# A hybrid decoder layer on one core: low halves of w_up and w_down formed by an accumulating transfer

## The chip, the core and the metric

One core of one Trainium2 chip. The metric is the device time of one execution in microseconds; the kernel before takes 1103.26 us (median of 2 runs, 1103.16 to 1103.37).

## What is computed

One layer on 256 tokens of width 2048, all in float32: a pooling mixer and sparse attention, an output projection, and a gated feed-forward network with a causal convolution of width 3. The part that the change touches is the last:

```python
def conv_ffn(h, w_up, conv_w, conv_b, w_down):      # w_up 2048 x 11264, w_down 5632 x 2048
    up = h @ w_up
    ...
    c = conv_b + sum(conv_w[j] * up_p[:, j:j + S] for j in range(CONV_WIDTH))
    gate, val = jnp.split(c, 2, axis=-1)
    return (jax.nn.silu(gate) * val) @ w_down
```

## The kernel before

Every weight and every activation is split into a high half, its value rounded to the narrower float32r, and a low half, the difference. A product is the sum of high x high, low x high and high x low. The weights come as a stream of 384 pieces of mostly [128, 1024] float32 (512 KB), two to a unit that one transfer from SP loads into a tile `raw` (1 MB, two buffers). `Piece.split` makes the halves: ACT copies `raw` into `whi`, rounding (L103), DVE subtracts `whi` from `raw` into `wlo` (L104). Both have four buffers, so the halves of piece n use the buffers of piece n-4 and have to wait until that piece's products are done.

The main loop (L735 to L744) goes through the pieces in order. At step i it asks for the load of the unit of piece i+3, splits piece i+2 (`prep`), does the side work of the step (L740) and then the products of piece i. A framework turns this order into one instruction list for each engine, with semaphores between them; it may put instructions of one engine into another order than the code has, as long as the data allow it. Each engine works through its list in order, and so does the queue of transfers that SP issues.

The pieces from G0 = 120 to 295 are w_up: for each f of 44 a unit of gate columns and a unit of value columns, four pieces in all; products at L211 and L212. Side work in each round of four pieces: `up_out` takes the sums out of the accumulators (L613 to L615), `up_conv` does the convolution and the Silu (L623 to L626), `up_gate` forms the gated value and its halves (L631 to L633). The pieces from D0 = 296 to 383 are w_down, 44 units, with the same product lines (for the last two blocks of outputs L216 to L218) and nearly no side work. GpSimd has nothing to do in either stage but the norm's small steps at the start of w_up.

Of the kernel before, what the change touches and what calls it, by code (L numbers as in the profile page):

```python
# [11 lines left out]
AF = mybir.ActivationFunctionType  # L12
ALU = mybir.AluOpType
AX = mybir.AxisListType

P = 128
S = 256
# [10 lines left out]

# columns of the packed parameters
C_AG, C_FG, C_PS, C_QG, C_KG, C_IC, C_CW, C_CB = 0, 16, 32, 40, 41, 42, 58, 58 + 3 * 2 * NF  # L30
C_N = C_CB + 2 * NF

# the indexer's columns: heads (with the key and the head weights in the first chunk)
IHEADS = (5, 6, 5)
IWIDTH = (5 * 64 + 80, 6 * 64, 5 * 64)
# pool groups, the widest window first
GROUPS = (3, 2, 1, 0)
# the columns of w_in: indexer, keys, queries, values, pool groups
ORDER = ("i0", "i1", "i2", "k0", "k1", "u0", "q0", "q1", "u1", "v0", "u2", "v1", "u3")
# [4 lines left out]
def hybrid_kernel(ctx, tc, xT, par, wI0, wI1, wI2, wA, wU, wP, wO, wUp, wDn, out):  # L44
    nc = tc.nc
# [11 lines left out]

# [1 line left out]
    warm = cp.tile([P, 512], BF16, name="warm")  # L59
# [8 lines left out]
    nc.gpsimd.memset(ones, 1.0)  # L68
    # loads the table of functions
    tab = cp.tile([P, 1], F32, name="tab")  # L70
# [3 lines left out]

# [1 line left out]
    class Unit:  # L76
        """Columns of weights that are loaded together."""

# [3 lines left out]
        def load(self):  # L82
            if self.raw is None:
                self.raw = wp.tile([P, 2048], F32, name="raw", tag="raw", bufs=2)
                for i, (a, b) in enumerate(self.cuts):
                    if i == 1 and self is pieces[0].unit:
                        nc.scalar.dma_start(ga, par[:, C_AG:C_AG + KT])
                        nc.sync.dma_start(xf[:, 0:2], xT[:, 0:2])
                    nc.sync.dma_start(self.raw[:, a:b], self.src[:, a:b])

    class Piece:
        """Columns a .. b of a unit, split together, and the products that use them."""

        def __init__(self, unit, a, b, mm):
            self.unit, self.a, self.b, self.mm = unit, a, b, mm

        def split(self, parts=1):
            self.hi = wp.tile([P, 1024], F32R, name="whi", tag="whi", bufs=4)
            self.lo = wp.tile([P, 1024], F32R, name="wlo", tag="wlo", bufs=4)
            n = (self.b - self.a) // parts  # L100
            for c in range(0, n * parts, n):
                raw, hi = self.unit.raw[:, self.a + c:self.a + c + n], self.hi[:, c:c + n]
                i1 = nc.scalar.activation(hi, raw, AF.Copy)  # L103
                i2 = nc.vector.tensor_tensor(self.lo[:, c:c + n], raw, hi.bitcast(F32), op=ALU.subtract)  # L104
                self.issued = i1.ins, i2.ins
# [4 lines left out]
    pieces = []  # L110
    sides = {}

    def at(step, f, *a):
        sides.setdefault(step, []).append(lambda: f(*a))

# [1 line left out]
    def split_x(k, src, gains, on_act):  # L117
# [16 lines left out]

# [1 line left out]
    def rsqrt_cols(pool, src, n, mul, name):  # L136
# [6 lines left out]
    class TokenNorm:  # L143
        """From a [P, S] sum of squares over features: r by token, as columns and along rows."""

# [27 lines left out]
    def squares(q):  # L173
        # not ahead of the first pieces
        act, dve = pieces[7].issued
        with tc.issue_after(act), tc.issue_after(dve):
            nc.scalar.activation(sqz[:, 0], xf[:, 4 * q:4 * q + 4], AF.Square)
            nc.vector.tensor_reduce(sqz[:, 1, q], sqz[:, 0].rearrange("p k t -> p t k"), axis=AX.X, op=ALU.add)  # L178
# [3 lines left out]

# [1 line left out]
    class Acc:  # L184
        """Accumulators [P, 2, 512] or [P, 512], taken when the first product is traced."""

# [10 lines left out]
    def mm_tok(acc, piece, ks, width):  # L197
        """tokens on partitions: acc[:, th, :width] += x[:, k].T @ w[k]."""
        pt = acc.get()
        for i, k in enumerate(ks):  # L200
            wh, wl = piece.get(i * width, width)
            for th in range(2):
                t = slice(th * P, (th + 1) * P)
                o = pt[:, th, :width]
                nc.tensor.matmul(o, xhl[:, k, 0, t], wh, start=(k == 0), stop=False)  # L205
                nc.tensor.matmul(o, xhl[:, k, 0, t], wl, start=False, stop=False)  # L206
                nc.tensor.matmul(o, xhl[:, k, 1, t], wh, start=False, stop=(k == KT - 1))  # L207

    def mm_feat(o, wh, wl, rhs, first, last):
        """features on partitions: o[:, 0:256] += w.T @ hi, + wl.T @ hi; o[:, 256:512] += wh.T @ lo."""  # L210
        nc.tensor.matmul(o, wh, rhs.rearrange("p a t -> p (a t)"), start=first, stop=False)  # L211
        nc.tensor.matmul(o[:, 0:S], wl, rhs[:, 0], start=False, stop=last)  # L212

    def mm_feat1(o, wh, wl, rhs, first, last):
        """The same, all in o[:, 0:256]."""
        nc.tensor.matmul(o[:, 0:S], wh, rhs[:, 0], start=first, stop=False)  # L216
        nc.tensor.matmul(o[:, 0:S], wh, rhs[:, 1], start=False, stop=False)  # L217
        nc.tensor.matmul(o[:, 0:S], wl, rhs[:, 0], start=False, stop=last)  # L218

    def tok_chunk(srcs, width, cuts=()):  # L220
        """16 k-tiles of `width` columns, in units of 4 and pieces of 2 k-tiles."""
        acc = Acc()
        for q in range(4):
            u = Unit(srcs[q], 4 * width, cuts[q] if q < len(cuts) else None)
            for h in range(2):
                def mm(p, k0=4 * q + 2 * h):
                    mm_tok(acc, p, (k0, k0 + 1), width)
                pieces.append(Piece(u, 2 * h * width, (2 * h + 2) * width, mm))
        return acc

    # ================= the stream of pieces =================
    def pool_chunk(n):
# [12 lines left out]
    ia, za, ua, first = [], {}, [], {}  # L245
    W = IWIDTH[0]
    for name in ORDER:
        first[name] = len(pieces)
        if name[0] == "i":
            c = int(name[1])  # L250
            src = (wI0, wI1, wI2)[c]
# [4 lines left out]
        else:  # L256
            c = ("k0", "k1", "q0", "q1", "v0", "v1").index(name)
            za[name] = tok_chunk([wA[c, q] for q in range(4)], 512)

    # rows of w_out: heads 0 .. 3, the first pool groups, heads 4 .. 7, the last pool group  # L260
    yhl = zc.tile([P, KT, 2, S], F32R, name="yhl")
# [27 lines left out]
    G0 = len(pieces)  # L289
# [14 lines left out]
    D0 = len(pieces)  # L304
    ghl = None
    for i in range(16 * NF // 8):
# [10 lines left out]
        o = (i % 2) * 1024  # L317
        pieces.append(Piece(u, o, o + 1024, mm))

    # ================= indexer =================  # L320
    qiT = [zc.tile([P, 8, S], F32R, name=f"qiT{c}", tag="big", bufs=2) for c in range(2)]
# [43 lines left out]
    def tr_iq(h0):  # L365
        """Heads h0 and h0 + 1: [hi; lo] on partitions."""
        tp = ps_s.tile([P, 512], F32, name="tp", tag="ss")
        for a in range(2):
            st, h = qst[h0 + a]
            for th in range(2):  # L370
                nc.tensor.transpose(tp[:, (a * 2 + th) * P:(a * 2 + th + 1) * P],  # L371
                                    st[:, th, h].rearrange("p a d -> p (a d)").bitcast(F32), ident)
        nc.scalar.activation(qiT[h0 // 8][:, h0 % 8:h0 % 8 + 2].rearrange("p a t -> p (a t)"), tp, AF.Copy)
# [33 lines left out]

    # ================= attention =================
    gqk = zc.tile([P, 1], F32, name="gqk")
# [101 lines left out]

    # ================= pool channels: features on partitions =================
    pw_ = {}
# [62 lines left out]

    # ================= x1, its norm =================
    sq1 = cp.tile([P, 2, S], F32, name="sq1")
# [16 lines left out]

    # ================= ConvFFN =================
    fw = {}
# [50 lines left out]

    # ================= what else happens at each piece =================
    at(9, nc.sync.dma_start, pr, par)  # L650
# [58 lines left out]

    # ================= the kernel =================  # L710
    def load(n):
# [11 lines left out]
    def prep(n):  # L723
        if 0 < n < 8:
            for k in (2 * n, 2 * n + 1):
                split_x(k, xf[:, k], ga, True)
        if n < len(pieces):
            pieces[n].split(2 if n == 0 else 1)
        if n == 0:
            for k in range(2):  # L730
                split_x(k, xf[:, k], ga, False)
# [3 lines left out]
    for i, p in enumerate(pieces):  # L735
        if i + 3 < 8:
            load_x(2 * (i + 3))
        load(i + 3)
        prep(i + 2)
        for f in sides.get(i, []):  # L740
            f()
        p.mm(p)
# [59 lines left out]
```

## Time and profile before

| | |
|---|---|
| median of the runs | 1103.26 us |
| span of the profiled execution | 1102.1 us |
| PE busy | 1092.7 us, 99% |
| DVE busy | 734.4 us, 67% |
| ACT busy | 570.0 us, 52% |
| POOL busy | 13.7 us, 1% |
| bytes read from HBM | 201.15 MB |
| granted PE clock | 1.00 throughout |

The profile is one execution, 1.2 us shorter than the median of the runs. A busy time is the sum of the spans of an engine's instructions, so PE, whose matmuls overlap, can be busy without being at its peak. The waits and the order in time say which engine another one waited for; a name such as `wlo` is a tile of the program, and L104 a line of it.

### The profile page before, as it was taken

The page shows a single profiled execution, that of the slowest core. Times are in us where ns is not written, and L with a number is a line of the kernel's source. Part 1 is how long each engine was busy: PE and PEld are TensorE (multiplying, and loading weights), DVE is VectorE, ACT ScalarE, POOL GpSimd, SP SyncE. Part 2 cuts the span into 40 slices and gives each one's busy share as a digit, 9 for nine tenths or more (in the row PEclk, how much of TensorE's full clock was granted, in tenths as well). Part 3 has the DMA queues.
Part 4 walks back from the last instruction along what each step waited for, and adds up shares of the span by engine and source line. Part 5 has one row for each costly group of instructions (what it writes and reads, how often), then busy time and mean ns, then how long its engine had stood idle before and what let it go on. Part 6 is the DMA issues. An engine that isn't in the chain of part 4 may idle for free.

```text
span 1102.1 us, 16427 instructions
## 1 busy us (share of the span) xinstructions
PE 1092.7 (99%) x6620; PEld 974.2 (88%) x6620; DVE 734.4 (67%) x1034; ACT 570.0 (52%) x792; POOL 13.7 (1%) x25
## 2 busy tenths in 40 slices
PE   8999999999999999999999999999999999999998
PEld 6998989889999988888888888888888888888898
DVE  7767867665556677777877787878777544444442
ACT  6555456654444555555555555555555433344441
POOL 0001000000000000000000000000000000000000
PEclk9999999999999999999999999999999999999999
DMA  7554554444555555555555555555555555555552
GB/s 261 165 179 163 191 202 156 163 162 161 181 191 174 175 192 187 191 191 191 191 192 191 191 191 191 192 191 191 190 192 188 188 198 200 197 199 196 198 197 76
DMA packets 31755, 204.30 MB, mean 185 GB/s; under 512 B 3648, under 2 KB 4288, under 8 KB 8640
## 3 DMA queue, kind: packets, MB, share of 16 engines
q1 hardware_dynamic: 30240, 201.16, 53.4%
q10 hardware_dynamic: 1440, 2.11, 0.5%
q8 instruction: 52, 0.85, 0.3%
q14 instruction: 23, 0.19, 0.0%
HBM read 201.15 MB, written 2.10 MB: 184 GB/s over the span
## 4 chain that ended last, share of the span: by engine, by line
PE 96%; DVE 1%; DMA 1%; issue 1%; ACT 0%; SPq 0%; ACTq 0%; DVEq 0%
PE mm L211 43%; PE mm L212 21%; PE mm L218 5%; PE mm L217 5%; PE mm L216 5%; PE mm L206 5%; PE mm L205 5%; PE mm L207 5%; DMA raw<-in_wI_dram 1%; DVE wlo L104 1%; PE sp L381 1%; PE sp L467 0%; DVE sqz L178 0%; PE tp L455 0%; PE tp L371 0%
## 5 line engine op out<-in xcount | busy, mean ns | idle before, releaser
L104 DVE TENSOR_TENSOR wlo<-raw,whi 128x1024 fp32r<-128x1024 f32 (+4 forms) x385 | 462.1, 1202 | 297.4 <-ACT whi L103 297.3
L103 ACT ACTIVATE whi<-raw 128x1024 fp32r<-128x1024 f32 (+4 forms) x385 | 399.9, 1041 | 428.8 <-PE mm L211 260.4
L211 PE MATMUL mm<-xhl,whi 128*128 128x512 f32 x1408 | 488.5, 394 | 0.0
L212 PE MATMUL mm<-xhl,wlo 128*128 128x256 f32 x1408 | 390.1, 277 | 0.0
L211 PEld LDWEIGHTS mm<-xhl,whi 128*128 128x128 f32 x1408 | 264.0, 188 | 61.3
L212 PEld LDWEIGHTS mm<-xhl,wlo 128*128 128x128 f32 x1408 | 264.2, 188 | 0.0
L211 PE MATMUL mm<-ghl,whi 128*128 128x512 f32 x616 | 213.6, 394 | 0.0
L212 PE MATMUL mm<-ghl,wlo 128*128 128x256 f32 x616 | 170.6, 277 | 0.0
L211 PEld LDWEIGHTS mm<-ghl,whi 128*128 128x128 f32 x616 | 115.5, 188 | 26.9
L212 PEld LDWEIGHTS mm<-ghl,wlo 128*128 128x128 f32 x616 | 115.6, 188 | 0.0
L205 PE MATMUL mm<-whi,xhl 128*128 128x512 f32 (+3 forms) x288 | 108.6, 377 | 2.3 <-ACT xhl L120 0.8
L206 PE MATMUL mm<-wlo,xhl 128*128 128x512 f32 (+3 forms) x288 | 107.0, 371 | 2.5 <-DVE wlo L104 2.4
L207 PE MATMUL mm<-whi,xhl 128*128 128x512 f32 (+3 forms) x288 | 106.8, 371 | 0.0
L216 PE MATMUL mm<-yhl,whi 128*128 128x256 f32 x256 | 72.6, 284 | 0.0
L218 PE MATMUL mm<-yhl,wlo 128*128 128x256 f32 x256 | 72.4, 283 | 0.0
L217 PE MATMUL mm<-yhl,whi 128*128 128x256 f32 x256 | 72.4, 283 | 0.0
L206 PEld LDWEIGHTS mm<-wlo,xhl 128*128 128x128 f32 x288 | 54.1, 188 | 10.7 <-DVE wlo L104 4.0
L205 PEld LDWEIGHTS mm<-whi,xhl 128*128 128x128 f32 x288 | 54.1, 188 | 10.5 <-ACT whi L103 1.8
L207 PEld LDWEIGHTS mm<-whi,xhl 128*128 128x128 f32 x288 | 54.1, 188 | 8.3 <-DVE xhl L123 0.5
L217 PEld LDWEIGHTS mm<-yhl,whi 128*128 128x128 f32 x256 | 49.1, 192 | 0.0
L216 PEld LDWEIGHTS mm<-yhl,whi 128*128 128x128 f32 x256 | 49.1, 192 | 0.0
L218 PEld LDWEIGHTS mm<-yhl,wlo 128*128 128x128 f32 x256 | 49.1, 192 | 0.0
(155 smaller groups left out, 928.9 us busy)
## 6 DMA issues: line engine op xcount, KB each, us to landing
raw<-in_wUp_dram SPq DMA_DIRECT2D x88, 1024.0 KB, 4.8
raw<-in_wDn_dram SPq DMA_DIRECT2D x44, 1024.0 KB, 4.8
raw<-in_wA_dram SPq DMA_DIRECT2D x24, 1024.0 KB, 4.8
raw<-in_wO_dram SPq DMA_DIRECT2D x16, 1024.0 KB, 4.8
raw<-in_wU_dram SPq DMA_DIRECT2D x8, 1024.0 KB, 4.8
raw<-in_wI_dram SPq DMA_DIRECT2D x4, 768.0 KB, 4.2
raw<-in_wI_dram SPq DMA_DIRECT2D x7, 400.0 KB, 5.2
raw<-in_wI_dram SPq DMA_DIRECT2D x4, 640.0 KB, 4.1
```

The lines of the kernel that those rows point to most:

```text
L103: i1 = nc.scalar.activation(hi, raw, AF.Copy)
L104: i2 = nc.vector.tensor_tensor(self.lo[:, c:c + n], raw, hi.bitcast(F32), op=ALU.subtract)
L205: nc.tensor.matmul(o, xhl[:, k, 0, t], wh, start=(k == 0), stop=False)
L206: nc.tensor.matmul(o, xhl[:, k, 0, t], wl, start=False, stop=False)
L207: nc.tensor.matmul(o, xhl[:, k, 1, t], wh, start=False, stop=(k == KT - 1))
L211: nc.tensor.matmul(o, wh, rhs.rearrange("p a t -> p (a t)"), start=first, stop=False)
L212: nc.tensor.matmul(o[:, 0:S], wl, rhs[:, 0], start=False, stop=last)
L216: nc.tensor.matmul(o[:, 0:S], wh, rhs[:, 0], start=first, stop=False)
L217: nc.tensor.matmul(o[:, 0:S], wh, rhs[:, 1], start=False, stop=False)
L218: nc.tensor.matmul(o[:, 0:S], wl, rhs[:, 0], start=False, stop=last)
L381: nc.tensor.matmul(sp[:, a:b], q, kiT[:, e, 0:b - a], start=(e == 0), stop=(e == 1))
```

## The change

For every piece n from G0 to D0 + 87 with n mod 4 = 1 (44 of w_up, 22 of w_down; called adder pieces below) the subtraction on DVE is left out. ACT instead writes the negated, rounded copy of `raw` into `wlo`, and GpSimd issues a transfer that adds the float32 weights onto it. For w_up the source of the transfer is `raw` in SBUF, for w_down the same columns in DRAM, read a second time. In the main loop an adder piece is split one step earlier than the others (at step n-3), and before that split the load of the following unit is asked for. Comments of the file are removed as well; those lines are left out here.

```diff
-            self.unit, self.a, self.b, self.mm = unit, a, b, mm
+            self.unit, self.a, self.b, self.mm, self.adder = unit, a, b, mm, None
...
                 i1 = nc.scalar.activation(hi, raw, AF.Copy)
+                if self.adder:
+
+                    nc.scalar.activation(self.lo[:, c:c + n], raw, AF.Copy, scale=-1.0)
+                    src = raw
+                    if self.adder == "dram":
+                        src = self.unit.src[:, self.a + c:self.a + c + n]
+                    nc.gpsimd.dma_start(self.lo[:, c:c + n], src, accum_op=ALU.add)
+                    continue
                 i2 = nc.vector.tensor_tensor(self.lo[:, c:c + n], raw, hi.bitcast(F32), op=ALU.subtract)
...
+    for n in range(G0, D0 + 88):
+        if n % 4 == 1:
+            pieces[n].adder = "sbuf" if n < D0 else "dram"
...
         load(i + 3)
-        prep(i + 2)
+
+        if not (i + 2 < len(pieces) and pieces[i + 2].adder):
+            prep(i + 2)
+        if i + 3 < len(pieces) and pieces[i + 3].adder:
+            load(i + 4)
+            prep(i + 3)
```

## Rows read from the trace of the kernel before

**Rows 1.** The page: span, then busy us and share of each engine.
```profile
span 1102.1 us, 16427 instructions
PE 1092.7 (99%) x6620; PEld 974.2 (88%) x6620; DVE 734.4 (67%) x1034; ACT 570.0 (52%) x792; POOL 13.7 (1%) x25
```
**Rows 2.** Busy us by engine in two stretches, clock, DMA share, GB/s.
```profile
core 0: us, PE busy (x) PEld busy (x) DVE busy (x) ACT busy (x) POOL busy (x), PEclk, DMA share, GB/s
...
354.00:832.00 478.00, 478.00 (x2789) 419.27 (x2788) 362.46 (x511) 272.01 (x385) 1.77 (x3) 1.00 0.55 189
832.00:1095.00 263.00, 263.00 (x1592) 233.42 (x1590) 134.12 (x132) 107.67 (x115) 0.00 (x0) 1.00 0.55 188
```
**Rows 3.** Waits of PE, longest group: us in total, times, longest us.
```profile
PE mm L206 <- DVE wlo L104: 2.4, 4, 1.3
```
**Rows 4.** Line 211: duration ns min/median/max, first and last start us.
```profile
L211 PE MATMUL mm<-xhl,whi x1408: 391/395/476, 364.3 to 853.0; 128*128 128x512 f32 x176
...
L211 PE MATMUL mm<-ghl,whi x616: 392/394/396, 853.4 to 1066.6; 128*128 128x512 f32 x154
```
**Rows 5.** Groups by line, 380 to 1102 us: busy us, mean ns, idle before.
```profile
L104 DVE TENSOR_TENSOR wlo<-raw,whi 128x1024 fp32r<-128x1024 f32 x256 | 313.5, 1225 | 206.9 <-ACT whi L103 206.9
L103 ACT ACTIVATE whi<-raw 128x1024 fp32r<-128x1024 f32 x256 | 271.1, 1059 | 284.0 <-PE mm L211 256.4 <-DMA raw<-in_wUp_dram 13.8 <-PE mm L217 10.2
```
**Rows 6.** ACT in order of time in w_up: start us, us, instruction, idle before.
```profile
598.38 1.06 ACT L103 ACTIVATE whi<-raw 128x1024 fp32r<-128x1024 f32 x1 [1.49 <-PE mm L211]
599.35 0.58 ACT L613 ACTIVATE ft<-mm 128x512 f32<-128x512 f32 x1
601.50 1.06 ACT L103 ACTIVATE whi<-raw 128x1024 fp32r<-128x1024 f32 x1 [1.58 <-DMA raw<-in_wUp_dram]
602.47 1.08 ACT L623 ACTIVATE fc<-up,pr 128x256 f32<-128x256 f32 x2
603.93 1.06 ACT L103 ACTIVATE whi<-raw 128x1024 fp32r<-128x1024 f32 x1 [0.38 <-PE mm L211]
```
**Rows 7.** DVE in the same stretch: the subtraction of the second half.
```profile
605.32 1.22 DVE L104 TENSOR_TENSOR wlo<-raw,whi 128x1024 fp32r<-128x1024 f32 x1
```
**Rows 8.** Loads issued on SP's queue: start us, us of the issue.
```profile
595.18 0.33 SPq L89 DMA_DIRECT2D raw<-in_wUp_dram  x1
...
606.57 0.33 SPq L89 DMA_DIRECT2D raw<-in_wUp_dram  x1
```
**Rows 9.** Transfers by line: count, KB each, median us from issue to landing.
```profile
raw<-in_wUp_dram SPq DMA_DIRECT2D x88, 1024.0 KB, 4.8
...
raw<-in_wI_dram SPq DMA_DIRECT2D x4, 768.0 KB, 4.2
...
out_dram<-ft ACTq DMA_DIRECT2D x7, 256.0 KB, 3.1
...
out_dram<-ft ACTq DMA_DIRECT2D x2, 128.0 KB, 1.8
```
**Rows 10.** The page: SP's queue, packets, MB, share of 16 engines' span.
```profile
q1 hardware_dynamic: 30240, 201.16, 53.4%
```
**Rows 11.** Single microseconds of w_up; the last two columns are DMA share, GB/s.
```profile
603.00:604.00 1.00, 1.00 (x7) 0.89 (x6) 1.00 (x2) 0.62 (x3) 0.00 (x0) 1.00 1.00 426
...
605.00:606.00 1.00, 1.00 (x7) 0.87 (x7) 1.00 (x3) 0.42 (x1) 0.00 (x0) 1.00 0.02 8
```
**Rows 12.** ACT in order of time in w_down, two of a repeating row.
```profile
903.39 1.06 ACT L103 ACTIVATE whi<-raw 128x1024 fp32r<-128x1024 f32 x1 [1.71 <-PE mm L211]
906.16 1.06 ACT L103 ACTIVATE whi<-raw 128x1024 fp32r<-128x1024 f32 x1 [1.71 <-PE mm L211]
```

## The prediction

> **What bounds the kernel now.** I read the busy table first. TensorE (PE) is busy 1092.7 of the 1102.1 us, VectorE (DVE) 67%, ScalarE (ACT) 52%, GpSimd (POOL) 1% [rows 1]. A busy PE is not yet a PE that sets the end, so next come the stretches: from 354 to 832 and from 832 to 1095 us, nearly all of the w_up and w_down stages, PE's busy time equals the stretch to a hundredth, at clock 1.00 [rows 2]. The waits of PE say the same from the other side: its longest group is four waits for a low half, 2.4 us in all [rows 3], and the two stretches hold none of them [rows 2]. So in the two stages that the change touches PE waits for nobody, and the most that a relieved DVE could give back anywhere is 1102.1 - 1092.7 = 9.4 us, 0.9%.
>
> That sets PE's pace. The first product of w_up starts at 364.3 us, the first of w_down at 853.4 [rows 4]: 489.1 us for 176 pieces, 2.78 us a piece, 11.1 us for a round of four. Adder pieces come once a round.
>
> Then I looked for the reserve: how early a piece's halves are made. On ACT a high half takes 1.06 us, the next instruction begins 0.97 us after it began [rows 5, 6]. The copy at 603.93 us is that of the second half of a w_up unit whose first half was copied at 601.50. It had waited for the products four pieces earlier to give its buffer back; its own products begin three pieces later, 603.93 + 3 x 2.78 = 612.3, about. The reserve is 8.3 us, and the old path (copy, then a subtraction that ends at 606.54) uses 2.6 of it [rows 6, 7].
>
> Last, the raw buffers. There are two, and units take turns. SP issues the load of a unit as soon as the subtraction of the unit two before it is done: 606.57 against 606.54 us [rows 7, 8]. A 1 MB load lands 4.8 us after its issue in the median [rows 9]; the one issued at 595.18 landed only as the copy at 601.50 began, 6.3 us later [rows 6, 8]. So a raw buffer goes round load, copy, copy, subtract, load, and this round also comes once in 11.1 us. It is the round that the change lengthens.
>
> **The change, part by part.** *Removed:* 66 subtractions of 1.225 us, 81 us of DVE [rows 5]. In these stages no PE wait names DVE, so this buys nothing.
>
> *Added on ACT:* 66 negated copies of the size of the high-half copy: 66 x 1.06 = 70 us. ACT is busy 272 of 478 us in the w_up stretch [rows 2]; one copy a round makes it about 318. Hidden behind PE as throughput, but it stands in the chain below.
>
> *Added on POOL and the DMA engines:* 66 transfers of 512 KB that read the source, read minus the high half, and write the sum. POOL does next to nothing else in these stages. The engines have room as an average: SP's queue takes 53.4% of them [rows 10]. A load runs in bursts (share 1.00 and 426 GB/s in one microsecond, 8 GB/s two later [rows 11]), so a transfer that falls into a burst is delayed.
>
> *Moved:* an adder piece is split a step earlier and the load of the next unit goes ahead of it on SP. The copies cannot come earlier for that: at 603.93 us ACT was already waiting for PE to release the buffer [rows 6]. What the move does is put copy, copy, negated copy side by side, and keep the other unit's load from queueing behind the transfer.
>
> *The price D of one transfer, issue to landing.* The trace has no accumulating transfer and none issued by POOL, so I bound it. Loads of 768 and 1024 KB land in 4.2 and 4.8 us [rows 9]: 0.6 us per 256 KB, hence 4.8 - 2 x 0.6 = 3.6 us for a plain 512 KB. That is the low end. If the two reads cost what reading 1 MB costs, D = 4.8. If the read of the destination comes first and the rest after it, two plain transfers, D = 7.2; three, with the write apart, 10.8, the high end. I take D = 6.0, midway between 4.8 and 7.2.
>
> The Trainium skill, DMA: Bandwidth & Descriptors, section Anatomy of one DMA — SWDGE (gpsimd) path, fits 2.0 us plus bytes over 436 GB/s; the estimate for 512 KB is 3.2 us, by which the w_up sum below would be 9 us instead of 132. It speaks for the change, and no run shown here has such a transfer. Collectives: The Full Stack (the Trainium skill again), section The bandwidth ceiling, says that a reduction in the DMA engines costs its second read, not its addition; with 1 MB in the same fit the estimate is 4.4 us, and the w_up sum 62 us; no row here shows that either.
>
> *w_up, source in SBUF, 44 rounds.* Here the transfer reads raw, so the raw buffer is free only when it has landed, and the load behind it on SP waits that long; behind that load waits the other unit's load too. The round of the buffer: load 4.8, copies 0.97 + 0.97 + 1.06 = 3.0, three hand-overs of about 0.1 (SP's was 0.03 [rows 7, 8]), transfer D: 8.1 + D. PE's round is 11.1. With D = 6.0 the buffer's round is 14.1 and PE stands 3.0 us in each: 44 x 3.0 = 132 us. The first round eats a reserve of a few microseconds, which I leave out. The two loads go out back to back and are done before the transfer starts, so I add no contention here.
>
> *w_down, source in DRAM, 22 rounds.* Raw is free after the negated copy, at about the old time, so the buffer's round is 8.1 us and hidden. What remains is the reserve: copies for piece n begin when piece n-4 is done (ACT waits 1.71 us each time for just that, every 2.77 us [rows 12]), then 0.97 + 1.06 + 0.2 + D must fit into the 8.3 us until piece n is due: D up to 6.0 is hidden. But the next load is released by the same negated copy and starts beside the transfer. Alone a load keeps the engines for 1 MB / 342 GB/s = 3.1 us (342 = 201.16 MB / (0.534 x 1102.1 us) [rows 1, 10]); the transfer loses between none and all of that; I take half, 1.5. It is then late by 2.2 + 6.0 + 1.5 - 8.3 = 1.4 us: 22 x 1.4 = 31 us.
>
> *Sum* against the profiled execution: 1102.1 + 132 + 31 = 1265; the median of the runs is 1.2 above it: **1266 us**, 15% slower.
>
> **The rivals.** *Not slower: the transfer is short.* One place decides: the raw buffer's round. At D = 3.0 or less it closes within 11.1 us and the time stays 1103. Up to D = 3.5 the loss is 44 x 0.5 = 22 us, which is 2%, about what a measurement of this kernel can tell from no change. For it: a 256 KB store lands in 3.1 us, a 128 KB store in 1.8 [rows 9]. Against it: every load of more than that takes over 4 us, and this one moves 512 KB and reads twice.
>
> *It costs a plain copy.* D = 3.6: the round is 11.7, 44 x 0.6 = 26, w_down hidden: 1130 us. This is what the second read being free would mean. The skill's fit of DMA: Bandwidth & Descriptors, named above, says so or less.
>
> *It is a chain of passes.* D from 7.2 to 10.8, at 9.0: 44 x 6.0 + 22 x (2.2 + 9.0 + 1.5 - 8.3) = 264 + 97, 1464 us; at 10.8 with full contention 44 x 7.8 + 22 x 7.8 = 515, 1618 us. For it: no row prices what POOL does to issue such a transfer, nor how reads and write of one row overlap; against it: the engines moved up to 426 GB/s [rows 11].
>
> Two costs inside these cases: if the two conv steps of L623, 1.08 us together, stand between the ACT copies, as they did at 602.47 [rows 6], 44 x 1.1 = 48 us more; and stops of 3 us could lower PE's clock, which with waits of at most 1.3 us [rows 3] no row shows. In w_up PE is not in the round and has room for it; in w_down a piece at 1.2 instead of 2.4 GHz would add up to 2.8 x 22 = 62 us.
>
> **How the numbers follow.** Transfer of 4.8 to 7.2 us (forecast): 0.55, own range 1185 to 1345 (44 x 1.8 + 22 x 0.2, and 44 x 4.2 + 22 x 2.6). Plain copy to 4.8: 0.12. Chain of passes: 0.20. Short: 0.13, of which 0.01 for a gain beyond 2%, which 9.4 us of PE idle exclude unless the profile misleads. I leave the short case out below and the far third of the chains above (0.07): 1130 to 1500. Faster 0.01, same 0.12, slower 0.87.
>
> **What would show it.** Right: SP's queue in w_up waits for the transfer, ACT waits for a load before the first copy of a unit, PE waits for wlo about 3 us once per four pieces in w_up and less in w_down; issue to landing of the transfers near 6 us. DVE falls by some 81 us, ACT rises by 70. Wrong: D below 3.5 us, or PE waiting as long in w_down as in w_up, which would mean that the transfer itself and not the raw buffer sets the round.

## The result and the profile after

The changed kernel takes 1244.4 us (median of 2 runs), 1.128 times the time before, 95% interval 1.126 to 1.130. The forecast was 1266. The profiled execution spans 1242.7 us, 140.6 more than before.

The page of the changed kernel, busy us and share by engine, the queue of the new transfers, and the chain that ended last:

```profile
span 1242.7 us, 16490 instructions
PE 1130.2 (91%) x6620; PEld 993.1 (80%) x6620; DVE 665.3 (54%) x968; ACT 632.4 (51%) x858; POOL 69.1 (6%) x91
...
q0 software_dynamic: 9504, 34.61, 14.3%
...
DMA 42%; PE 37%; ACT 9%; issue 6%; DVE 4%; SPq 0%; ACTq 0%; DVEq 0%
```

DVE lost 69 us and ACT gained 62 against [rows 1], as the edit says, and neither mattered. The chain that ended last is now made of transfers (loads and additions), 42% of it; before, 96% of it was PE.

The two stretches (w_up, w_down) of the changed kernel; columns as in [rows 2]:

```profile
364.30:937.90 573.60, 517.01 (x2827) 442.33 (x2826) 330.00 (x485) 321.34 (x440) 38.24 (x47) 0.97 0.64 202
937.90:1238.90 301.00, 254.30 (x1496) 222.30 (x1495) 92.19 (x88) 115.45 (x118) 17.92 (x21) 0.99 0.67 191
```

w_up took 489.1 us before [rows 4] and takes 573.6: 84.5 more, 1.92 for each of 44 rounds. w_down went from 245.4 (853.4 to the end of the products) to 301.5: 56.1 more, 2.55 for each of 22. Together 140.6: all of the loss is here, and PE, which had been busy through both stretches, has gaps in both (56.6 and 46.7 us). The rest of the loss is inside PE's busy time, 1130.2 us against 1092.7 for the same 6620 products.

The waits of PE, and of SP's queue in w_up (us in total, times, longest us):

```profile
PE mm L220 <- DMA wlo<-raw: 56.6, 35, 3.1
PE mm L220 <- DMA wlo<-in_wDn_dram: 43.1, 19, 3.4
```

```profile
SPq L89 <- DMA wlo<-raw: 509.1, 43, 13.5
```

PE waits for the transferred low halves: with 3.6 us more at the last lines of w_down, 103.3 us in all. SP, which had waited for subtractions, waits in w_up for transfers, once a round. One round of w_up shows the whole loop; first ACT, then the transfers that POOL issues, then SP's load (start us, us, instruction, what ended the idle time before it):

```profile
606.57 2.01 ACT L103 ACTIVATE whi<-raw 128x1024 fp32r<-128x1024 f32 x2 [1.64 <-DMA raw<-in_wUp_dram]
608.49 1.04 ACT L106 ACTIVATE wlo<-raw 128x1024 fp32r<-128x1024 f32 x1
...
620.57 2.01 ACT L103 ACTIVATE whi<-raw 128x1024 fp32r<-128x1024 f32 x2 [2.92 <-DMA raw<-in_wUp_dram]
```

```profile
609.82 0.86 POOL L110 DMA_DIRECT2D wlo<-raw  x1 [11.88 <-ACT wlo L106]
623.82 0.84 POOL L110 DMA_DIRECT2D wlo<-raw  x1 [13.14 <-ACT wlo L106]
```

```profile
601.64 0.80 SPq L89 DMA_DIRECT2D raw<-in_wUp_dram  x2
...
615.61 0.33 SPq L89 DMA_DIRECT2D raw<-in_wUp_dram  x1
```

Load issued 601.64, copies from 606.57 (4.9 us), negated copy done 609.53 (3.0), transfer issued 609.82 (0.3), next load issued 615.61 as it landed (5.8): 14.0 us. Most rounds are 12.5 to 13.1, with a transfer of 4.3 to 5.0; in nine of the 44, one in five, it lands late like this one, after 5.4 to 6.1 us, and the mean of the 44 is 4.7. Why it does is open. ACT waits for the load before the first copy; its waits for the loads of w_up come to 74.4 us, against 13.8 before [rows 5].

The transfers, KB and median us from issue to landing:

```profile
raw<-in_wUp_dram SPq DMA_DIRECT2D x88, 1024.0 KB, 5.1
raw<-in_wDn_dram SPq DMA_DIRECT2D x44, 1024.0 KB, 5.8
...
wlo<-raw POOLq DMA_DIRECT2D x44, 512.0 KB, 4.4
...
wlo<-in_wDn_dram POOLq DMA_DIRECT2D x22, 512.0 KB, 8.3
```

So D, taken as 6.0 in the forecast, is 4.4 from SBUF with the engines to itself and 8.3 beside loads. The last transfer of w_down, which no load follows, lands in 5.6.

One round of w_down: ACT, the transfer, SP's loads, and PE's wait for the piece:

```profile
1000.97 1.06 ACT L103 ACTIVATE whi<-raw 128x1024 fp32r<-128x1024 f32 x1 [3.84 <-PE mm L219]
1001.93 1.04 ACT L106 ACTIVATE wlo<-raw 128x1024 fp32r<-128x1024 f32 x1
```

```profile
1003.27 0.86 POOL L110 DMA_DIRECT2D wlo<-in_wDn_dram  x1 [12.31 <-ACT wlo L106]
```

```profile
1003.00 0.33 SPq L89 DMA_DIRECT2D raw<-in_wDn_dram  x1
...
1008.80 0.33 SPq L89 DMA_DIRECT2D raw<-in_wDn_dram  x1
```

```profile
1012.08 0.39 PE L220 MATMUL mm<-ghl,wlo 128*128 128x256 f32 x1 [2.54 <-DMA wlo<-in_wDn_dram]
```

The copy waits for PE to give back the buffer of the piece four before. The transfer, issued at 1003.27, lands 8.8 us later, and PE has waited 2.5 us for it. Not one but two loads run beside it: the one issued 0.3 us before it, and the next, issued at 1008.80. So it is with every transfer of the stage but the last.

### The profile page after: what moved, and what is told of

Read it like the earlier page. It is cut to its first block, busy times and chain, and to the rows that moved or that the text cites. A ratio compares the mean times of both kernels' runs of the same rounds, so it can differ in the third digit from the quotient of the medians.

```text
span 1242.7 us, 16490 instructions
## 1 busy us (share of the span) xinstructions
PE 1130.2 (91%) x6620; PEld 993.1 (80%) x6620; DVE 665.3 (54%) x968; ACT 632.4 (51%) x858; POOL 69.1 (6%) x91
## 4 chain that ended last, share of the span: by engine, by line
DMA 42%; PE 37%; ACT 9%; issue 6%; DVE 4%; SPq 0%; ACTq 0%; DVEq 0%
DMA raw<-in_wUp_dram 15%; DMA wlo<-in_wDn_dram 12%; DMA wlo<-raw 12%; PE mm L219 6%; ACT whi L103 5%; PE mm L226 4%; PE mm L224 4%; PE mm L225 4%; PE mm L214 4%; PE mm L213 4%; PE mm L215 4%; ACT wlo L106 4%; PE mm L220 4%; DVE wlo L112 3%; DMA raw<-in_wDn_dram 2%
## 5 line engine op out<-in xcount | busy, mean ns | idle before, releaser
L112 DVE TENSOR_TENSOR wlo<-raw,whi 128x1024 fp32r<-128x1024 f32 (+4 forms) x319 | 381.0, 1197 | 446.4 <-ACT whi L103 445.2
L103 ACT ACTIVATE whi<-raw 128x1024 fp32r<-128x1024 f32 (+4 forms) x385 | 394.0, 1037 | 393.9 <-PE mm L219 162.8
L219 PE MATMUL mm<-xhl,whi 128*128 128x512 f32 x1408 | 507.4, 403 | 0.0
L220 PE MATMUL mm<-xhl,wlo 128*128 128x256 f32 x1408 | 404.8, 288 | 56.6 <-DMA wlo<-raw 56.6
L220 PEld LDWEIGHTS mm<-xhl,wlo 128*128 128x128 f32 x1408 | 272.4, 193 | 68.4 <-DMA wlo<-raw 68.2
L219 PEld LDWEIGHTS mm<-xhl,whi 128*128 128x128 f32 x1408 | 270.7, 192 | 62.8
L220 PE MATMUL mm<-ghl,wlo 128*128 128x256 f32 x616 | 175.2, 284 | 43.1 <-DMA wlo<-in_wDn_dram 43.1
L631 ACT ACTIVATE fc<-up,pr 128x256 f32<-128x256 f32 x88 | 48.1, 594 | 94.0 <-DVE up L623 94.0
L110 POOL DMA_DIRECT2D wlo<-raw x44 | 37.6, 854 | 638.6 <-ACT wlo L106 624.9
L106 ACT ACTIVATE wlo<-raw 128x1024 fp32r<-128x1024 f32 x66 | 68.8, 1042 | 0.0
```

The source lines that it names most:

```text
L106: nc.scalar.activation(self.lo[:, c:c + n], raw, AF.Copy, scale=-1.0)
L631: nc.scalar.activation(c[:, j], u[:, j, 2:], AF.Identity, bias=pr[:, C_CB + n:C_CB + n + 1], scale=cw[2])
```

## Experiments

My theory has two loops. In w_up raw is held until the transfer has landed, so the buffer's round (load, copies, transfer, next load) sets the pace. In w_down raw is free early; the reserve of 8.3 us runs out because the next load is released with the transfer and shares the engines. There the late piece also gives its buffer back late, the copies four pieces later start late in turn, and so the delay recurs in every round. The rivals: the transfer is just too slow or its presence too costly; the early split does harm; freeing raw would be the cure; the lowered clock is a large part.

Stage lengths, from the first product of w_up to the first of w_down, and from there to the start of DVE's last addition for the output (us; in brackets the difference to before). e1, e2, e3, e7 and e8 were run once, the others two to ten times; the stages are those of one profiled execution each:

| | time | w_up | w_down |
|---|---|---|---|
| before | 1103.3 | 489.1 | 245.4 |
| changed | 1244.4 | 573.6 (84.5) | 301.5 (56.1) |
| e1_up_only | 1191.0 | 572.3 (83.2) | 249.5 (4.1) |
| e2_down_only | 1154.0 | 489.1 (0) | 296.2 (50.8) |
| e3_move_only | 1103.2 | 489.1 (0) | 245.5 (0) |
| e4_every8 | 1159.3 | 514.1 (25.0) | 275.6 (30.2) |
| e5_neg_first | 1246.8 | 567.5 (78.4) | 308.4 (63.0) |
| e6_down_sbuf | 1222.3 | 566.7 (77.6) | 290.1 (44.7) |
| e7_plain | 1137.1 | 510.7 (21.6) | 256.9 (11.5) |
| e8_free_raw | 1351.5 | 683.3 (194.2) | 299.0 (53.6) |
| e9_neg_first | 1182.8 | 537.4 (48.3) | 277.9 (32.5) |
| e10_half | 1133.3 | 506.2 (17.1) | 258.5 (13.1) |
| e11_filler | 1328.8 | 654.6 (165.5) | 306.0 (60.6) |
| e12_half_first | 1111.7 | 497.4 (8.3) | 249.5 (4.1) |

Builds differ by some microseconds for no reason that is known: w_up of e6 has the code of the changed kernel and is 7 us shorter.

**One stage alone, and the order alone.**

```diff
-    for n in range(G0, D0 + 88):
+    for n in range(G0, D0):          # e1_up_only
+    for n in range(D0, D0 + 88):     # e2_down_only
...
-                if self.adder:
+                if False:                # e3_move_only
```

> The change in w_up alone: its 44 pieces form the low half by a transfer, the 22 of w_down subtract on DVE as before. In the changed kernel the w_up stage grew from 489.1 to 573.6 us. Buffer-round theory (raw is held until the transfer has landed): w_up 573 to 575 us, w_down back to 245, time 1188, within 4. Rival, the two stages load each other (the transfers' issue on GpSimd, queue state): time more than 8 us away from that.

> The change in w_down alone (22 transfers, source in DRAM). Theory: in w_down it is the reserve that runs out, beside a load that starts with the transfer: w_down stays 56 us longer than before, w_up 489, time 1159, within 4; transfers land in 8 us. Rival, the slowdown of w_down is inherited from a late w_up: time under 1145.

> The same order of the main loop (adder pieces split a step earlier, next load ahead of them), but their low half subtracted on DVE as before. Theory: the order alone costs nothing, 1103, within 3. Rival, the early split itself delays other work on ACT or the loads: 1115 or more.

1191.0, 1154.0 and 1103.2 us. Each stage loses by itself what it loses in the changed kernel, to 1 and 5 us; w_down's loss is not handed on from w_up, and the order costs nothing. e2 came out 5 us below its expectation. A third thing shows in e1: w_down is 4 us longer without a transfer in it. PE is busy for 249.5 of 249.9 us there, at clock 1.00, so it waits for nobody and the products themselves take 1.7% longer; why is open.

**Every second round without a transfer.**

```diff
-        if n % 4 == 1:
+        if n % 8 == 1:
```

> Adder pieces only where n mod 8 = 1: 22 in w_up and 11 in w_down, every second round. Buffer-round theory: the raw buffer loses 2 us in a round with a transfer and has 3 us to spare in the next (8.1 against 11.1), so w_up loses nearly all of its stops: 489 to 497 us; in w_down each transfer is late by itself, half of 56 us. Time 1131 to 1139. Rival, each transfer is simply too slow for its own piece, in w_up too: half of 84.5 and half of 56, time 1173.

1159.3 us, between the two forecasts. In w_down half the transfers cost half (30.2 of 56.1), as theory and rival both had it. In w_up each now costs 1.14 us, not near 0 and not 1.92. The trace of this build says why (ACT, one round with a transfer):

```profile
614.95 1.06 ACT L103 ACTIVATE whi<-raw 128x1024 fp32r<-128x1024 f32 x1 [3.26 <-DMA raw<-in_wUp_dram]
615.92 1.08 ACT L631 ACTIVATE fc<-up,pr 128x256 f32<-128x256 f32 x2
616.90 1.05 ACT L103 ACTIVATE whi<-raw 128x1024 fp32r<-128x1024 f32 x1
618.49 0.42 ACT L634 ACTIVATE fc<-fc 128x256 f32<-128x256 f32 x1 [0.54 <-DVE fc L633]
618.82 1.04 ACT L106 ACTIVATE wlo<-raw 128x1024 fp32r<-128x1024 f32 x1
```

The framework put two convolution steps and a Silu between the copies, so from first copy to end of negated copy it is 4.9 us instead of 3.0. From this transfer's issue (620.15) to the next one's (643.52) two rounds pass: transfer 4.55, load 4.9, copies and subtraction 3.8, load 4.9, copies and conv steps 4.9, hand-over 0.3: 23.4 us, and two of PE's rounds are 22.2. The loop of the buffer adds up to the time, the spare round gives back what it should; my number for it was too good because I had reckoned with ACT's order in the changed kernel.

**An earlier start of the transfer.** The first try changed only the order in the source, the second also held the high half's copy back. The lines are those of e9; e5 has no `with` line.

```diff
-                i1 = nc.scalar.activation(hi, raw, AF.Copy)
                 if self.adder:
...
+                    neg = nc.scalar.activation(self.lo[:, c:c + n], raw, AF.Copy, scale=-1.0)
...
                     nc.gpsimd.dma_start(self.lo[:, c:c + n], src, accum_op=ALU.add)
+                    with tc.issue_after(neg.ins):
+                        nc.scalar.activation(hi, raw, AF.Copy)
                     continue
```

> In adder pieces ACT writes the negated copy first, so that the transfer starts one copy (0.97 us) earlier and the high half is copied beside it. Theory: the transfer's start is a link of both rounds, so each of the 66 rounds loses 0.97 us: w_up 84.5 - 43 = 42 us over before, w_down 56 - 21 = 35, time 1180. Rival, the engines that move the data are what is short: nothing is gained by an earlier start, 1235 or more.

> As e5_neg_first, but with the high half of an adder piece held behind its negated copy on ACT, since in e5 the framework had put both back into the old order. In w_down, where ACT does little else, the transfer starts 0.97 us earlier: theory, 22 x 0.97 = 21 us less than in the changed kernel. In w_up the Silu of the convolution now stands between the first half's copy and the negated copy, so 0.4 to 0.7 us a round are left: 18 to 29 us less. Time 1194 to 1206. Rival, the movers and not the start set the pace: 1235 or more.

e5 took 1246.8 us and tested nothing: in its trace ACT still does the adder piece's copy (L110) ahead of its negated copy (L105).

```profile
604.06 1.06 ACT L112 ACTIVATE whi<-raw 128x1024 fp32r<-128x1024 f32 x1 [0.77 <-DMA raw<-in_wUp_dram]
605.02 1.05 ACT L110 ACTIVATE whi<-raw 128x1024 fp32r<-128x1024 f32 x1
605.97 1.04 ACT L105 ACTIVATE wlo<-raw 128x1024 fp32r<-128x1024 f32 x1
```

e9, where the order is held, took 1182.8 us: w_down 23.6 shorter than in the changed kernel (21 expected), w_up 36 shorter (18 to 29 expected), with transfers that land in 4.4 and 8.0 us as before. An earlier start of just under one microsecond is passed on almost whole in all 66 rounds. That is how a loop behaves, and not how a shortage of transfer rate would.

**The source of the transfer.**

```diff
-            pieces[n].adder = "sbuf" if n < D0 else "dram"
+            pieces[n].adder = "sbuf"                         # e6_down_sbuf
...
-                    src = raw
+                    src = xf[:, 0:4]                         # e8_free_raw, w_up
```

> In w_down too the transfer reads raw in SBUF, so the next load waits until it has landed and no longer runs beside it. Theory: transfers land in 4.4 us instead of 8.3, and it is then the buffer's round of 13.0 us that counts, 1.9 to 2.1 us too long: w_down 42 to 46 us over before, time 1230 to 1236. Rival, a w_down without conv work on ACT closes the round in time: 1190. Rival, no raw hold can be cheaper than contention: over 1245.

> In w_up the transfer's source is another 512 KB in SBUF (the residual stream) instead of raw; raw is free after the copies, and the sum is not the low half. If holding raw were the only cost of w_up, the w_up stage would fall to 489 us and the time to 1160. Theory: the next load then starts with the transfer and the two share the engines as in w_down, where a lone transfer took 5.6 us and one beside a load 8.4: landing in 7 to 8 us, 1.3 to 2.3 us too late for its piece, w_up 60 to 100 us over before, time 1219 to 1260; SP waits for no transfer.

e6: 1222.3 us, below the expected 1230 to 1236, but w_down itself, 44.7 us over before, is where it was expected (42 to 46). Most of the rest is w_up's 7 us. The median landing of all 66 transfers is 4.4 us there: with the load made to wait, the contention is gone and the buffer's round is what counts.

e8 is the telling one. SP waits for no transfer any more, raw is free as early as before, and w_up is not 489 us long but 683, far above the 60 to 100 us that I expected on top. The transfers of e8, one round of ACT, PE's clock in the microseconds after a stop, and two rounds as a whole (columns as in [rows 2]):

```profile
wlo<-xf POOLq DMA_DIRECT2D x44, 512.0 KB, 9.0
```

```profile
718.74 1.06 ACT L103 ACTIVATE whi<-raw 128x1024 fp32r<-128x1024 f32 x1 [3.27 <-PE mm L222]
...
734.66 1.06 ACT L103 ACTIVATE whi<-raw 128x1024 fp32r<-128x1024 f32 x1 [4.74 <-PE mm L222]
```

```profile
730.00:731.00 1.00, 0.53 (x3) 0.52 (x4) 1.00 (x4) 0.00 (x0) 0.00 (x0) 1.00 0.93 385
731.00:732.00 1.00, 1.00 (x6) 0.85 (x5) 0.78 (x2) 0.00 (x0) 0.00 (x0) 0.67 0.51 213
732.00:733.00 1.00, 1.00 (x5) 0.89 (x4) 0.00 (x0) 0.00 (x0) 0.00 (x0) 0.50 0.08 33
```

```profile
706.79:721.35 14.56, 11.38 (x66) 9.75 (x65) 7.40 (x11) 7.27 (x11) 0.84 (x2) 1.00 0.66 181
721.35:737.27 15.92, 12.92 (x65) 10.98 (x64) 7.40 (x11) 7.26 (x11) 0.85 (x1) 0.89 0.60 165
```

The copies at 718.74 and 734.66 each wait for the products of an adder piece to give back its buffer; 15.9 us lie between them. Copy, a Silu and negated copy take it to 721.35, the transfer, beside loads issued at 721.08 and 726.73, 9.0 us to 730.4, and then the adder piece runs at half clock and takes 4.2 us instead of 2.8. Once the copies wait for the late piece itself, PE is part of the loop, and the clock that falls after a stop (the row of 732 shows 0.50, 1.2 GHz) lengthens it: the round before, at 1.00 throughout, took 14.6 us, this one 15.9. Both are far over 11.1, so the late transfer is the larger part. Holding raw, which I had as the cause of w_up's loss, thus also spares it something worse: the transfer runs with the engines to itself.

**The price of the transfer.**

```diff
-                    nc.gpsimd.dma_start(self.lo[:, c:c + n], src, accum_op=ALU.add)
+                    nc.gpsimd.dma_start(self.lo[:, c:c + n], src)      # e7_plain
```

> The same transfers without the addition: a plain copy of the weights over the negated half (the low half is wrong then; the work on all engines is otherwise the same). If the second read costs a pass over the data, w_up's transfers land 1.5 us earlier than 4.4, at about 2.9, and w_up is 66 us shorter than 573.6, which brings it near 508; time 1244 - 66 - 20 = 1158. If the second read is free, the transfers still land in 4.4 us and the time stays 1244. Halfway: 1200.

e7 took 1137.1 us. Its queue and its transfers:

```profile
q0 software_dynamic: 9504, 34.61, 8.4%
...
wlo<-raw POOLq DMA_DIRECT2D x44, 512.0 KB, 3.1
```

From SBUF 3.1 us instead of 4.4, from DRAM beside loads 5.9 instead of 8.3. The engines were busy 0.084 x 1135.4 / 66 = 1.45 us for one, with the addition 0.143 x 1242.7 / 66 = 2.69. The addition nearly doubles the engines' time, as a second pass over the data would. The 1.5 us expected of it were 1.3 in landing time, but the plain transfer's round is 4.9 + 3.0 + 0.3 + 3.1 + 0.1 = 11.4, 0.3 above PE's, and w_up came within 3 us of the expected 508; w_down gained 45 us where I had put 20, so the time came out 21 below the expected 1158.

**Half the size, and both shortenings.**

```diff
+                    m = n // 2
+                    lo, s0 = self.lo[:, c:c + m], self.a + c
+                    nc.scalar.activation(lo, raw[:, 0:m], AF.Copy, scale=-1.0)
+                    src = raw[:, 0:m]
...
+                    nc.gpsimd.dma_start(lo, src, accum_op=ALU.add)
+                    nc.vector.tensor_tensor(self.lo[:, c + m:c + n], raw[:, m:n], hi[:, m:n].bitcast(F32),
+                                            op=ALU.subtract)
```

These are the lines of e10; e12 also holds the high half's copy behind the negated copy, as e9 does.

> Each of the 66 transfers forms only the first 512 columns of its low half (256 KB); DVE subtracts the rest. A transfer of 512 KB took the engines 2.7 us of its 4.4; half of it should land in 3.1. Theory: w_up's round is 4.95 + 0.97 + 0.4 (Silu) + 0.97 + 0.55 + 0.3 + 3.1 + 0.1 = 11.3, 9 us over before in 44 rounds; w_down's transfer beside a load lands in 5.5 to 7 and needs at most 6.5: 0 to 15 us. Time 1112 to 1127. Rival, what costs is that a transfer is there at all (its issue, its semaphore), not its length: 1200 or more.

> Both shortenings at once: the transfer forms half of the low half (256 KB), and its negated copy of 512 columns goes ahead of the high half's copy. Theory: w_up's round is 4.95 + 0.97 + 1.1 (the conv step now stands there) + 0.5 + 0.3 + 3.2 + 0.1 = 11.1, level with PE's 11.1: 0 to 6 us over before; w_down needs 0.6 + 0.3 + 6.5 = 7.4 of 8.3 us, hidden. Time 1103 to 1109, the time before, with 66 transfers still in place. Rival, a cost of the transfers beside the two rounds (engines, GpSimd, the lowered clock): 1120 or more, near the 1133 of the half transfers alone.

e10: 1133.3 us, 6 above the expected span, with w_up 17 over before (9 expected) and w_down 13. Its transfers land in 3.2 and 6.5 us. e12: 1111.7 us, 1.006 times the time before (1.004 to 1.009); its single runs lie between 1104 and 1116, and the profile is of the longest of them. Its transfers, PE's wait for them, and its two stages (columns as in [rows 2]):

```profile
wlo<-raw POOLq DMA_DIRECT2D x44, 256.0 KB, 3.2
wlo<-in_wDn_dram POOLq DMA_DIRECT2D x22, 256.0 KB, 4.1
```

```profile
PE mm L225 <- DMA wlo<-raw: 0.6, 2, 0.4
```

```profile
364.20:861.60 497.40, 496.85 (x2827) 431.57 (x2826) 342.85 (x526) 296.55 (x439) 38.26 (x47) 1.00 0.64 209
861.60:1111.08 249.48, 249.44 (x1497) 220.52 (x1496) 107.14 (x110) 106.83 (x120) 17.92 (x21) 1.00 0.67 208
```

With all 66 transfers in place PE waits 0.6 us for them, where it waited 103.3. Shortening the two loops gives back 133 of 141 us. The rest, 8 us in w_up and 4 in w_down of this longest run, is no wait: PE is busy through both stages at clock 1.00, and its products take 1.6 and 1.7% longer than before, as in w_down of e1. Why they do stays open.

**The clock.**

```diff
+        if p.adder:
+            pw = ps_s.tile([P, 512], F32, name="pw", tag="ss")
+            for _ in range(10):
+                nc.tensor.matmul(pw, warm[:, 0:P], warm, start=True, stop=True)
         p.mm(p)
```

> Ten idle matmuls (512 columns, about 2.2 us) in front of each adder piece's products, to fill the stop in which PE waits for the transfer. In the changed kernel the granted clock falls to 0.5 for some microseconds after a stop of 3 us (mean 0.985). Theory: the clock is off the path in w_up, where the raw buffer's round does not pass PE, and on it in w_down, where the next copies wait for the piece after the stop: w_up unchanged within 4 us, w_down 4 to 10 us shorter, time 1234 to 1240, mean clock 0.99 or more. Rival, the lowered clock is part of the loss everywhere: 1243 x 0.015 = 19 us, time 1225. Rival, the fillers themselves are late work: slower than 1244.

e11 took 1328.8 us and does not answer its question. The fillers changed the framework's order on ACT:

```profile
609.67 1.06 ACT L103 ACTIVATE whi<-raw 128x1024 fp32r<-128x1024 f32 x1 [4.95 <-DMA raw<-in_wUp_dram]
610.63 0.40 ACT L634 ACTIVATE fc<-fc 128x256 f32<-128x256 f32 x1
612.35 0.42 ACT L640 ACTIVATE ghl<-fc 128x256 fp32r<-128x256 f32 x1 [1.32 <-DVE fc L639]
612.68 1.04 ACT L103 ACTIVATE whi<-raw 128x1024 fp32r<-128x1024 f32 x1
613.63 1.04 ACT L106 ACTIVATE wlo<-raw 128x1024 fp32r<-128x1024 f32 x1
```

From the first copy to the end of the negated copy it is 5.0 us here, 2.0 more than in the changed kernel, and w_up's round grew by (654.6 - 573.6) / 44 = 1.84. That is one more sign that the buffer's round is w_up's pace, found by accident. In w_down the mean clock was 0.99 (0.99 in the changed kernel too) and the stage did not get shorter.

The trace of the changed kernel itself bounds the clock's price in w_down. Of its rounds, from transfer to transfer, only two hold a stretch at 0.50; the first of them and the round before it (columns as in [rows 2]):

```profile
1154.71:1167.91 13.20, 10.70 (x63) 9.19 (x62) 3.68 (x3) 5.22 (x6) 0.86 (x2) 1.00 0.71 199
1167.91:1183.12 15.21, 12.38 (x63) 10.52 (x62) 4.97 (x5) 5.37 (x6) 0.87 (x1) 0.89 0.66 191
```

The two took 15.2 and 15.0 us, the other 19 between 13.0 and 14.8, 13.6 in the mean. That makes about 3 of the 56 us, an estimate. What the clock costs in w_up was not measured.

## Why the prediction came out as it did

*PE bound, nothing to gain:* right. DVE's 69 us bought nothing.

*w_up, the raw buffer's round:* the mechanism was right. SP waits for 43 transfers, ACT for the load, and PE loses 1.9 us a round, 1.3 of it in waits; the round was put at 8.1 + D and the pieces measured are 4.9 + 3.0 + 0.3 + D + 0.1. The term that was mis-sized is D: 6.0 taken, midway between reading 1 MB and two transfers in a row, where the median was 4.4 and 4.8 had been my figure for reading as many bytes. By 4.4 the sum would have been 44 x 1.4 = 62 us, too low, because one round in five has a late transfer, which makes the mean 4.7, and the hand-over to POOL takes 0.3. With both, 44 x (8.3 + 4.7 - 11.1) = 84; 84.5 came out, 132 were forecast. The Trainium skill was nearer than I: by the fit of DMA: Bandwidth & Descriptors, section Anatomy of one DMA — SWDGE (gpsimd) path, with one read the estimate was 3.2 us, and e7's plain transfer took 3.1. With the second read, to which the Trainium skill, Collectives: The Full Stack, section The bandwidth ceiling, puts the price of a reduction, the estimate was 4.4, and the median measured was 4.4.

*w_down, the reserve beside a load:* right as a mechanism (e2, e6, and the lone last transfer of 5.6 us), too low in size. I reckoned with one load and half of its 3.1 us of engine time, 1.5. Two run beside the transfer, and they cost it 8.3 - 5.6 = 2.7 us; in e8, again beside two, it lost 9.0 - 4.4 = 4.6, more than the whole of one, which I had as the most. The landing of 8.3 instead of 7.5 makes 22 x (2.2 + 8.3 - 8.3) = 48 us; 56.1 were measured, 31 forecast. Of the 8 left over about 3 are the two rounds at a lowered clock; the rest was not shown.

*The sum:* 141 measured against 163, by two errors of opposite sign, 48 too much in w_up and 25 too little in w_down. That the total came so near is luck. The case given 0.55 was a transfer of 4.8 to 7.2 us; in w_up D was 4.4, 4.7 in the mean, which is the case given 0.12. Had the forecast taken the landings as measured without loads beside them, 4.4 and 5.6, its own sums would have given 62 + 22 and a time of 1187.

*The signs:* SP's and ACT's waits came as told; the landing was 4.4 instead of about 6 us, DVE fell by 69 instead of 81, ACT rose by 62 instead of 70. PE's waits came the other way round: about 3 us a round in w_up and less in w_down were forecast, 56.6 / 44 = 1.3 and (43.1 + 3.6) / 22 = 2.1 measured. That PE waits as long in w_down as in w_up was named as a sign that the transfer itself sets w_up's round. It was no such sign: SP's waits, the sum of e4's loop and e9 show the buffer's round in w_up, and w_down's waits are long because its transfer loses more to the loads than I had put.

*What I had not seen:* the order of ACT. Its price was listed as 48 us if conv steps came between the copies; in the changed kernel they did not; in e4 conv steps and a Silu did, in e11 a Silu and another copy, at 1.9 and 2.0 us a round. And that the hold of raw keeps load and transfer apart in w_up: I wrote that no contention had to be added there, but not that it would come as soon as raw was freed (e8).

*The rivals:* a chain of passes is out (D is 4.4 alone). A plain copy's price is out: 4.4 was measured where a plain one took 3.1 (e7). The short transfer, 3.5 us or less, is out with it; and its price was too low, since e7, with 3.1 us from SBUF, is 3% slower than before and its w_up 21.6 us longer, where the forecast's sum gives 44 x 0.1 = 4.

## What to carry to other kernels

An asynchronous transfer that reads a buffer holds it until it has landed; add its landing time to the round of that buffer and compare the round with the pace of the engine that sets the end, before asking whether the transfer is in time for its own reader. If a cure frees the buffer, look at what starts then: the next load may run into the very transfer. After each build read the order of the engine that feeds the loop, since the steps between two copies were worth 1.9 us a round in e4, more than halving the transfer, which took 1.2 off its landing.

## What the runs showed of the hardware

An accumulating transfer of 512 KB in SBUF took 4.4 us to land in the median against 3.1 for a plain one (e7), and 2.69 against 1.45 us of the engines; one of 256 KB took 3.2 (e10). Beside 1 MB loads one of 512 KB took 7.9 to 9.0 in the medians of the builds, from DRAM or (e8) from SBUF. POOL was occupied 0.85 us to issue one, 0.53 for a plain one.

PE's granted clock fell to 0.50 (1.2 GHz) at the end of a stop of 2.6 us in the changed kernel, was still 0.50 in the two rows from 616 to 618 with PE fully busy, and was 1.00 (2.4 GHz) again from 619 (columns as in [rows 2]):

```profile
613.00:614.00 1.00, 0.00 (x0) 0.00 (x0) 1.00 (x2) 0.00 (x0) 0.00 (x0) 1.00 0.72 139
...
616.00:617.00 1.00, 1.00 (x5) 0.81 (x5) 0.86 (x3) 0.20 (x1) 0.00 (x0) 0.50 0.83 123
...
619.00:620.00 1.00, 1.00 (x8) 0.86 (x7) 0.00 (x0) 0.00 (x0) 0.00 (x0) 1.00 1.06 442
```

It does so after some stops only; after the one near 1011 us in w_down it stayed at 1.00.
